# Two float32 blocks on one core: every second unit of weights is split by two loads instead of by DVE

## The chip, the cores and the metric

The kernel runs on one core of one Trainium2 chip. The metric is the device time of one execution in microseconds; the runs of a kernel are summed up by their median. One execution was recorded by the hardware profiler, and all rows below come from it.

## The reference

256 tokens of width 1024 go through two transformer-like blocks, all in float32:

```python
# first block
(q, kc, vc, ks, vs, kw, vw, nsa_g, rq, rk, rv, rg, gate_a, gate_b) = split(rmsnorm(x) @ w_in)
mix = sigmoid(gate_a) * (nsa_out @ w_proj_a) + sigmoid(gate_b) * (ret_out @ w_proj_b)
x = x + mix @ w_out
x = x + square(relu(rmsnorm(x) @ w_up)) @ w_down
x = rmsnorm(x)
# second block
h = x + hybrid_mixer(rmsnorm_2(x, ...), ...)          # SSD and gated linear attention
h = h + mem_cross_attention(rmsnorm_2(h, ...), rmsnorm_2(mem, ...), w_xq, w_xkv, w_xo)
h = h + swiglu(rmsnorm_2(h, ...), w_ffn_in, w_ffn_out)
return rmsnorm_2(h, norm_final)
```

Nearly all of the arithmetic is in the products with some 20 weight matrices, 163 MB in all, and every weight is used once for 256 tokens.

## The kernel before

TensorE multiplies operands of the type float32r, which has fewer bits than float32. So each float32 operand is split into two parts that are exact together: hi is the value rounded to float32r, lo is the value minus hi, rounded. A product of two operands takes three matrix products, hi x hi, hi x lo and lo x hi (the methods `tok_mm` and `feat_mm`, both through `mm`, line 104).

The weights come in 314 units of [128 partitions, 1024 columns], 512 KB (three of them smaller), which the host has laid out in `wbig` in the order of use. `load` (lines 87 to 97) fetches and splits one: SP's queue loads it into a buffer `raw` (line 93), ACT copies it to `wh` with rounding (line 94), and DVE subtracts `wh` from `raw` into `wl` (line 95). There are 4 buffers of `raw` and 8 each of `wh` and `wl`. So up to 8 units can be ready for TensorE and up to 4 more be on their way.

`gemm_tok` makes [128 tokens, 512 columns] from units of two blocks of 128 rows, once for each half of the tokens; `gemm_feat` makes [256 features, 256 tokens] from units of four blocks, and takes two units for 1024 rows, 48 matrix products. The `Down` class adds up the second matrix of an MLP, one unit for each 256 rows of it, 24 matrix products. The stages follow each other: the projections, the sparse attention (`nsa`) with other projections pumped in between, retention, the gated mix, the MLP of the first block (from 240 to 415 us), then the second block's projections, its two mixers, the cross attention, and its MLP to the end.

The activations are split in the same manner (`split`, line 111, ACT and then DVE). Before each of the large products stands a norm over the tokens: ACT squares and sums, DVE adds, GpSimd takes the power -1/2 (`rsqrt`, line 209), DVE scales, TensorE transposes, ACT and DVE split.

The order of the instructions on each engine is set when the program is built, by a scheduler with a model of the times; at run time each engine works off its own queue in order, and semaphores hold it where an operand isn't there yet. SP's queue holds nearly nothing but the 314 loads of weights. GpSimd's queue holds 27 loads (gains of the norms, the memory, decays, parameters), the powers of the norms, and some small operations. What `nc.gpsimd.dma_start` loads is moved by the same 16 DMA engines as SP's loads; GpSimd only issues it.

Of the kernel before, what the change touches and what calls it, by code (L numbers as in the profile page):

```python
# [19 lines left out]
P = 128  # L20
# [5 lines left out]
# columns of the packed constant array  # L26
C_ID, C_TRI, C_RST, C_INV, C_MC, C_AV, C_I94, C_BM, C_SEL, C_N = 0, 128, 256, 512, 584, 614, 616, 646, 654, 670
# packed parameters of the first block
A_PEK, A_PEV, A_CK2, A_CV2, A_N = 0, 16, 32, 288, 416
# packed parameters of the second block  # L30
B_CONV, B_BA, B_DTB, B_AL, B_D, B_A2, B_N = 0, 60, 64, 80, 96, 112, 624
# rows of gains
# [7 lines left out]
class Halves:  # L40
    """[128, 4 * n, 256 tokens], split in two exact parts, in tiles of four blocks each."""
# [8 lines left out]
class Builder:  # L50
# [35 lines left out]
    # ---- weights: loaded in units of up to half a megabyte, split into two parts that are exact together  # L86
    def load(self, w, c0, ncol, k, nk):
        nc = self.nc
        i = len(self.keys)
        self.keys.append((w, c0, ncol, k, nk))  # L90
        raw, wh, wl = self.T("raw", [P, UNIT]), self.T("wh", [P, UNIT], F32R), self.T("wl", [P, UNIT], F32R)
        m = nk * ncol
        nc.sync.dma_start(raw[:, :m], self.d["wbig"][i, :, :m])
        nc.scalar.copy(wh[:, :m], raw[:, :m])  # L94
        nc.vector.tensor_sub(wl[:, :m], raw[:, :m], wh[:, :m].bitcast(F32))  # L95
        cs = [slice(j * ncol, (j + 1) * ncol) for j in range(nk)]
        return [(wh[:, c], wl[:, c]) for c in cs]
# [23 lines left out]
    def gemm_tok(self, w, c0s, ncol, src, K=8, rest=None, mid=None, ahead=3, others=()):  # L121
        """[128 tokens, ncol] in one bank, for each group of columns and each half of the tokens; the first half of
        the tokens goes through all groups first, and rest makes the second half of src after that; mid takes the
        first half's results before the last group of the second."""
        us, n = [], UNIT // ncol
        for c0 in c0s:
            us.append([])
            for k in range(0, K, n):
                # all but the first weights are split after the first half of src
                with ExitStack() as order:  # L130
                    if rest and (c0 != c0s[0] or k >= ahead * n):
                        for x in self.first:
                            order.enter_context(self.tc.issue_after(x.ins))
                    us[-1] += self.load(w, c0, ncol, k, min(n, K - k))
                if c0 == c0s[0] and k // n in others:
                    others[k // n]()
# [10 lines left out]
    def s_tok(self, key, w, c0, ncol, src, done, K=8):  # L147
        """gemm_tok of one group of columns, in steps"""
# [17 lines left out]
    def s_feat(self, key, w, c0, src, done, K=8):  # L166
        """gemm_feat, in steps"""
# [18 lines left out]
    def gemm_feat(self, w, c0, src, K=8, tag="acc"):  # L186
        """[128 features, 2, 256 tokens]: two blocks of features in one bank."""
# [13 lines left out]
    def rstd(self, ssq, n, count, scale=1.0, eps=None):  # L201
        """1 / sqrt(scale * (ssq / count + eps))"""
# [9 lines left out]
    def norm_scale(self, src, junk):  # L212
        """1 / the root mean square of [128 tokens, 2 * 512]"""
# [7 lines left out]
    def norm_rows(self, src, g, out=None):  # L221
        """the norm of [128 tokens, 1024], in two tiles of 512 columns"""
# [8 lines left out]
    def norm_T(self, src, g, t, dst):  # L231
        """returns what is to be called for the transposes"""
# [7 lines left out]
    def norm_next(self, i, change):  # L240
        """the transposed norm of x as change leaves it, which calls its argument for each half of the tokens, and
        what is to be called for the second half of it"""
# [15 lines left out]
    def to_T(self, rows, t, dst, n=8, b0=0):  # L258
        """[128 tokens, n * 128] to the split [128, n, 128 tokens] at columns t."""
# [61 lines left out]
    def rope(self, out, x, t, nh, f0, nf, tmp):  # L321
        """out, x: [128 tokens, nh, 2, nf]; tmp [128, 2, nh, 2, nf]"""
# [15 lines left out]
    def compress(self, src, pe, w1, w2v, is_v):  # L338
        """src [128 = (token parity, dim), 2 groups, 256 tokens]"""
# [54 lines left out]
    def heads_T(self, kv, n, outs):  # L394
        """[128 tokens, n * 64]: each head, twice, transposed into the banks in outs"""
# [8 lines left out]
    def rope_T(self, acc):  # L404
        """rotary on four heads of 128, transposed: two tiles [128, 2 heads, 256 tokens]"""
# [21 lines left out]
    def silu2(self, acc, mul=None):  # L427
        """twice silu"""
# [24 lines left out]
    def nsa(self, hT, rest):  # L453
# [12 lines left out]
        # queries: two tiles of four heads; keys: [dim, branch, group, token]  # L466
# [12 lines left out]
        for t in range(2):  # L479
            ts = slice(t * P, (t + 1) * P)  # L480
            # keys and values of the compressed and the selected branch
# [13 lines left out]
            # queries  # L495
# [9 lines left out]
        for t in range(2):  # L505
            # window keys and values, gates
# [13 lines left out]
        # compressed attention  # L520
# [25 lines left out]
    def nsa_rest(self, kv_, gt, pcT, vbd):  # L546
        """selected and window attention, and the sum with the compressed one"""
# [140 lines left out]
    class Down:  # L688
        """x += u @ w: the blocks of u come one after the other, the last ones half of the tokens by half."""
# [15 lines left out]
        def rows(self, i, rows, scale):  # L705
            """four blocks, [128 tokens, 512] for each half of the tokens"""
# [11 lines left out]
        def feat(self, i, r, scale):  # L718
            """two blocks, [128 features, 2, 256 tokens]"""
# [4 lines left out]
        def go(self, n=1):  # L724
            """the products of the oldest blocks that wait"""
# [22 lines left out]
        def finish(self, then):  # L748
            """the rest, and then(t) for each half of the tokens"""
# [11 lines left out]
    def gated(self, gates, hT, aT, wa, Ka, bT, wb, Kb):  # L761
        """the split transpose of sigmoid(gate) * (a @ wa) + sigmoid(gate) * (b @ wb); the stream gives tanh(gate / 2)"""
# [22 lines left out]
    def residual(self, w, src, then):  # L785
        """x += src @ w, then(t) for each half of the tokens"""
# [8 lines left out]
    def dt_gate(self, hT, pb):  # L795
        """dt, its decays, and the transposed low-rank gate input."""
# [15 lines left out]
        # softplus: max(u, 0) + log1p(exp(-|u|)), log1p(e) = 2 atanh(e / (2 + e))  # L812
# [15 lines left out]
        # a = -exp(A_log) dt, its sums within each half, and their exponentials  # L828
# [21 lines left out]
        # the sums transposed, [head, token], in two parts that are exact together, one below the other  # L850
# [7 lines left out]
        # x, B and C come doubled  # L858
# [6 lines left out]
    def z_gate(self, hT, rest):  # L865
        """twice silu(z)"""
# [9 lines left out]
    def conv(self, pb, i, acc):  # L876
        """twice silu(conv(xBC)) for two blocks of features, [feature, 2, token]"""
# [42 lines left out]
    def ssd(self, hT, pb, dts, z, dec):  # L920
# [53 lines left out]
        def products(g, t, q):  # L974
# [18 lines left out]
            # the gate and the norm over the group  # L993
# [25 lines left out]
    def gla_decays(self, pb, a1T):  # L1019
        """exponentials of the sums of the log decays within chunks of 64 tokens, [dk, 2 heads, token], for each pair of  # L1020
        heads: for the queries, the keys, the keys towards the states, and each chunk's whole decay"""
# [11 lines left out]
        # one after the other, as they need another table  # L1033
# [18 lines left out]
    def gla(self, dec_):  # L1052
        """tiles of two chunks: the second chunk reads the first through their scores, and the second tile reads the
        first through one state"""
# [5 lines left out]
        for i in range(2):  # L1060
            v, r_ = self.need(f"v{i}"), self.need(f"r{i}")
            qt, kt, kh, dec = dec_[i]
            # scores, transposed: [key, head, query]
# [14 lines left out]
            # the state before the second tile, [dk, head, dv], and the queries that read it  # L1078
# [56 lines left out]
    def parts_of(self, src, scale=1.0, tags=("g2", "gd")):  # L1135
        """two tiles [128, 512] that make scale * src together"""
# [8 lines left out]
    def mm3(self, out, a, b, ca, cb, start, stop):  # L1145
        """out (+)= a[:, ca].T @ b[:, cb] of operands in two parts"""
# [110 lines left out]
def layout(inp):  # L1257
    """The inputs laid out for the loads; every value is copied as it is."""
# [91 lines left out]
```

## Time and profile before

| what | us |
|---|---|
| median of three runs (1007.6 to 1010.22) | 1008.44 |
| span of the profiled execution | 1007.4 |
| TensorE busy in it | 988.2 |
| DVE busy | 650.0 |
| ACT busy | 508.1 |
| GpSimd busy | 51.0 |

The profiled execution has no other time of its own than its span, from the first to the last instruction; it lies 1.0 us below the median of the runs. The granted clock of TensorE is at its full level from end to end (0.998 in the mean). 175.43 MB are moved by DMA, 174 GB/s in the mean, with the 16 DMA engines busy for about half of the time. Busy shares are read together with the list of waits: an engine that is busy for less than the span is late only where somebody waits for it.

### The profile page before, as it was taken

What the parts mean: (1) busy time and instruction counts of PE and PEld (TensorE: products, weight loads), DVE (VectorE), ACT (ScalarE), POOL (GpSimd) and SP (SyncE); (2) the same over time, 40 slices, a digit from 0 to 9 for tenths busy, and PEclk for the clock granted to TensorE, in tenths of its full rate; (3) what the DMA queues carried; (4) which work ended last, traced back from release to release, by engine and by line L of the source; (5) the groups of instructions that cost most, each with busy time, mean ns of one, the idle gap of its engine ahead of it and who ended that gap; (6) DMA issues with size and microseconds to landing.
All of it is one profiled execution on the core that took longest, in us unless ns stands there. A gap on an engine that the chain in (4) does not pass through costs nothing.

```text
span 1007.4 us, 16172 instructions
## 1 busy us (share of the span) xinstructions
PE 988.2 (98%) x6412; PEld 880.4 (87%) x6412; DVE 650.0 (65%) x959; ACT 508.1 (50%) x793; POOL 51.0 (5%) x77
## 2 busy tenths in 40 slices
PE   6999999999999999999999999999999999999997
PEld 5888998887888889789889899998998878999995
DVE  6897666666664555578778776576756466555543
ACT  5765445444554445465674555445545355444432
POOL 0000000000000000010000131200000000000000
PEclk9999999999999999999999999999999999999999
DMA  8758442333656575376445453753655156656531
GB/s 290 262 198 287 151 148 100 105 105 125 230 167 195 189 236 179 106 249 201 153 147 167 146 167 106 251 188 122 235 187 186 48 190 228 197 180 195 183 126 42
DMA packets 49547, 175.43 MB, mean 174 GB/s; under 512 B 5952, under 2 KB 6336, under 8 KB 49472
## 3 DMA queue, kind: packets, MB, share of 16 engines
q1 hardware_dynamic: 47088, 167.01, 50.5%
q0 software_dynamic: 2096, 6.87, 2.1%
q8 instruction: 50, 0.82, 0.3%
q10 hardware_dynamic: 288, 0.52, 0.1%
q14 instruction: 25, 0.20, 0.1%
HBM read 173.33 MB, written 1.05 MB: 173 GB/s over the span
## 4 chain that ended last, share of the span: by engine, by line
PE 96%; DMA 2%; ACT 1%; issue 1%; DVE 0%; SPq 0%; POOLq 0%; POOL 0%; ACTq 0%
PE acc L104 68%; PE sm L104 23%; PE sm L108 3%; PE po L104 2%; DMA raw<-in_wbig_dram 2%; ACT wh L94 1%; ACT hh L111 0%; DVE wl L95 0%; SPq L198 0%; SPq L276 0%; DVE k L1251 0%; ACT g L269 0%; POOLq L1344 0%; POOL sc L209 0%; SPq L280 0%
## 5 line engine op out<-in xcount | busy, mean ns | idle before, releaser
L95 DVE TENSOR_TENSOR wl<-raw,wh 128x1024 fp32r<-128x1024 f32 (+1 forms) x314 | 381.7, 1227 | 222.6 <-ACT wh L94 221.8
L94 ACT CAST wh<-raw 128x1024 fp32r<-128x1024 f32 (+1 forms) x314 | 325.6, 1048 | 304.3 <-PE acc L104 141.9
L104 PE MATMUL acc<-hh,wh 128*128 128x256 f32 x736 | 207.6, 283 | 0.4 <-ACT hh L111 0.4
L104 PE MATMUL acc<-hl,wh 128*128 128x256 f32 x736 | 207.8, 283 | 0.0
L104 PE MATMUL acc<-hh,wl 128*128 128x256 f32 x736 | 207.4, 282 | 0.0
L104 PE MATMUL acc<-wh,hh 128*128 128x512 f32 (+1 forms) x400 | 156.7, 397 | 1.9 <-ACT hh L111 1.9
L104 PE MATMUL acc<-wl,hh 128*128 128x512 f32 (+1 forms) x400 | 157.3, 395 | 0.0
L104 PE MATMUL acc<-wh,hl 128*128 128x512 f32 (+1 forms) x400 | 155.9, 397 | 0.0
L104 PEld LDWEIGHTS acc<-hh,wh 128*128 128x128 f32 x736 | 138.0, 188 | 1.7 <-ACT hh L111 0.5
L104 PEld LDWEIGHTS acc<-hl,wh 128*128 128x128 f32 x736 | 138.3, 188 | 0.9 <-issue 0.7
L104 PEld LDWEIGHTS acc<-hh,wl 128*128 128x128 f32 x736 | 138.1, 188 | 0.4 <-issue 0.3
L104 PE MATMUL sm<-hh,wl 128*128 128x256 f32 x488 | 136.4, 280 | 0.0
L104 PE MATMUL sm<-hl,wh 128*128 128x256 f32 x488 | 136.4, 279 | 0.0
L104 PE MATMUL sm<-hh,wh 128*128 128x256 f32 x488 | 136.2, 279 | 0.0
L104 PEld LDWEIGHTS acc<-wh,hh 128*128 128x128 f32 x400 | 75.8, 190 | 19.5 <-ACT hh L111 3.2
L104 PEld LDWEIGHTS sm<-hl,wh 128*128 128x128 f32 x488 | 91.6, 188 | 0.8
L104 PEld LDWEIGHTS sm<-hh,wh 128*128 128x128 f32 x488 | 91.5, 187 | 0.9
L104 PEld LDWEIGHTS acc<-wh,hl 128*128 128x128 f32 x400 | 75.7, 189 | 18.2 <-DVE hl L111 1.2
L104 PEld LDWEIGHTS sm<-hh,wl 128*128 128x128 f32 x488 | 91.5, 187 | 0.0
L104 PEld LDWEIGHTS acc<-wl,hh 128*128 128x128 f32 x400 | 75.7, 189 | 16.6 <-DVE wl L95 0.5
L104 PE MATMUL acc<-wh,gd 128*128 128x512 f32 x216 | 85.3, 396 | 1.6 <-ACT gd L699 1.2
L104 PE MATMUL acc<-wl,gd 128*128 128x512 f32 x216 | 84.8, 393 | 0.0
(272 smaller groups left out, 1058.0 us busy)
## 6 DMA issues: line engine op xcount, KB each, us to landing
raw<-in_wbig_dram SPq DMA_DIRECT2D x311, 512.0 KB, 4.0
k<-in_gains_dram POOLq DMA_DIRECT2D x18, 256.0 KB, 4.3
k<-in_mem_dram POOLq DMA_DIRECT2D x4, 256.0 KB, 6.4
raw<-in_wbig_dram SPq DMA_DIRECT2D x2, 420.0 KB, 3.8
k<-in_decay_dram POOLq DMA_DIRECT2D x4, 192.0 KB, 4.9
xr<-in_x_dram SPq DMA_DIRECT2D x2, 256.0 KB, 2.7
k<-in_gains_dram SPq DMA_DIRECT2D x2, 256.0 KB, 5.2
xr<-in_x_dram SPq DMA_DIRECT2D x1, 512.0 KB, 7.6
```

The costliest lines, as they stand in the source:

```text
L94: nc.scalar.copy(wh[:, :m], raw[:, :m])
L95: nc.vector.tensor_sub(wl[:, :m], raw[:, :m], wh[:, :m].bitcast(F32))
L104: self.nc.tensor.matmul(out, lhsT, rhs, start=start, stop=stop)
L108: self.nc.tensor.transpose(out, src, self.ident[:n, :n])
```

## The change

For the odd units from number 17 on, 149 of the 314, there is no `raw` buffer and nothing on SP's queue or on DVE. GpSimd's queue loads the unit straight into `wh`, a float32r tile, so that the load rounds. ACT then writes `wl` = -`wh`. After that GpSimd's queue loads the same unit from HBM a second time, with an addition: `wl` = `wl` + unit. The even units and the first 16 are fetched and split as before, and the matrix products are the same. (The comments and docstrings were also taken out of the file, and lines after `load` stand 8 lower.)

```diff
-        raw, wh, wl = self.T("raw", [P, UNIT]), self.T("wh", [P, UNIT], F32R), self.T("wl", [P, UNIT], F32R)
         m = nk * ncol
-        nc.sync.dma_start(raw[:, :m], self.d["wbig"][i, :, :m])
-        nc.scalar.copy(wh[:, :m], raw[:, :m])
-        nc.vector.tensor_sub(wl[:, :m], raw[:, :m], wh[:, :m].bitcast(F32))
+        src = self.d["wbig"][i, :, :m]
+        if i % 2 and i >= 16:
+
+            wh, wl = self.T("wh", [P, UNIT], F32R), self.T("wl", [P, UNIT], F32R)
+            nc.gpsimd.dma_start(wh[:, :m], src)
+            nc.scalar.activation(wl[:, :m], wh[:, :m].bitcast(F32), AF.Copy, scale=-1.0)
+            nc.gpsimd.dma_start(wl[:, :m], src, accum_op=OP.add)
+        else:
+            raw, wh, wl = self.T("raw", [P, UNIT]), self.T("wh", [P, UNIT], F32R), self.T("wl", [P, UNIT], F32R)
+            nc.sync.dma_start(raw[:, :m], src)
+            nc.scalar.copy(wh[:, :m], raw[:, :m])
+            nc.vector.tensor_sub(wl[:, :m], raw[:, :m], wh[:, :m].bitcast(F32))
```

The scheduler places the new instructions. On GpSimd before, from the loads of the gains for the norm ahead of the first MLP to the loads for the norms behind it (L198 loads gains, L209 is the power of a norm):

```order
L198 DMA k_532_2428<-in_gains_dram 128x512
L198 DMA k_533_2429<-in_gains_dram 128x512
L209 TENSOR_TENSOR sc_2569<-sc_2567,mhalf_74 128x1
L209 TENSOR_TENSOR sc_2620<-sc_2618,mhalf_74 128x1
L198 DMA k_832_4118<-in_gains_dram 128x512
L198 DMA k_833_4119<-in_gains_dram 128x512
```

On GpSimd now, at the two powers of that norm (L96 is the rounding load, L98 the accumulating load of the unit whose `wh` has the number one lower, L217 the power):

```order
L96 DMA wh_2599<-in_wbig_dram 128x1024
L98 DMA wl_2600<-in_wbig_dram 128x1024
L96 DMA wh_2610<-in_wbig_dram 128x1024
L217 TENSOR_TENSOR sc_2544<-sc_2542,mhalf_74 128x1
L98 DMA wl_2611<-in_wbig_dram 128x1024
L96 DMA wh_2621<-in_wbig_dram 128x1024
L96 DMA wh_2632<-in_wbig_dram 128x1024
L217 TENSOR_TENSOR sc_2595<-sc_2593,mhalf_74 128x1
L98 DMA wl_2622<-in_wbig_dram 128x1024
L98 DMA wl_2633<-in_wbig_dram 128x1024
```

Where GpSimd had the two powers alone, loads now stand before and between them, and the first accumulating load stands right behind the rounding load of its own unit. In the dense part of the same MLP, where GpSimd's queue was empty, it now holds:

```order
L96 DMA wh_3355<-in_wbig_dram 128x1024
L96 DMA wh_3397<-in_wbig_dram 128x1024
L98 DMA wl_3356<-in_wbig_dram 128x1024
L98 DMA wl_3398<-in_wbig_dram 128x1024
L96 DMA wh_3457<-in_wbig_dram 128x1024
L96 DMA wh_3499<-in_wbig_dram 128x1024
L98 DMA wl_3458<-in_wbig_dram 128x1024
L98 DMA wl_3500<-in_wbig_dram 128x1024
```

There two rounding loads stand side by side ahead of their two accumulating loads. ACT's queue in the same part (L94 and L102 round a unit of the old kind, L97 makes -`wh`, L676 and L684 are the relu of a group, L111 and L119 the rounding of its square), before:

```order
L94 CAST wh_3298<-raw_3297 128x1024
L94 CAST wh_3335<-raw_3334 128x1024
L94 CAST wh_3341<-raw_3340 128x1024
L94 CAST wh_3396<-raw_3395 128x1024
L94 CAST wh_3402<-raw_3401 128x1024
L676 ACTIVATE k_701_3327<-sm_3206 128x512
L111 CAST gd_3330<-k_701_3327 128x512
```

and now:

```order
L97 ACTIVATE wl_3254<-wh_3253 128x1024
L102 CAST wh_3301<-raw_3300 128x1024
L97 ACTIVATE wl_3296<-wh_3295 128x1024
L102 CAST wh_3361<-raw_3360 128x1024
L684 ACTIVATE k_662_3288<-sm_3169 128x512
L119 CAST gd_3291<-k_662_3288 128x512
L97 ACTIVATE wl_3356<-wh_3355 128x1024
```

Every second rounding copy has become a multiplication that waits for a load of GpSimd's queue.

## Rows read from the trace of the kernel before

**Rows 1.** The page, part 1: busy us (share of the span) and instructions by engine.

```profile
PE 988.2 (98%) x6412; PEld 880.4 (87%) x6412; DVE 650.0 (65%) x959; ACT 508.1 (50%) x793; POOL 51.0 (5%) x77
```

**Rows 2.** Waits of TensorE, longest first: us in total, times, longest us.

```profile
PE sm L108 <- DMA cst<-in_cst_dram: 7.9, 1, 7.9
PE acc L104 <- ACT hh L111: 2.2, 6, 0.8
```

**Rows 3.** Busy us by stretch: length, engines (instructions), clock, DMA share, GB/s.

```profile
core 0: us, PE busy (x) PEld busy (x) DVE busy (x) ACT busy (x) POOL busy (x), PEclk, DMA share, GB/s
0.00:50.00 50.00, 41.31 (x196) 34.23 (x197) 37.63 (x85) 34.41 (x57) 1.31 (x6) 1.00 0.81 276
50.00:100.00 50.00, 50.00 (x270) 42.41 (x269) 40.01 (x73) 31.60 (x56) 2.34 (x4) 1.00 0.72 242
...
250.00:300.00 50.00, 49.59 (x293) 43.45 (x293) 29.86 (x35) 26.56 (x36) 0.00 (x0) 1.00 0.61 204
300.00:400.00 100.00, 100.00 (x644) 90.49 (x643) 54.17 (x53) 46.02 (x53) 2.19 (x4) 1.00 0.63 204
400.00:450.00 50.00, 49.41 (x229) 39.88 (x228) 33.74 (x41) 26.33 (x42) 4.24 (x6) 1.00 0.51 164
450.00:500.00 50.00, 50.00 (x358) 45.39 (x357) 40.97 (x82) 29.99 (x48) 2.07 (x2) 1.00 0.60 188
...
600.00:650.00 50.00, 50.00 (x425) 48.45 (x424) 31.01 (x49) 25.48 (x40) 9.08 (x16) 1.00 0.55 184
...
700.00:750.00 50.00, 50.00 (x405) 48.89 (x405) 33.87 (x37) 26.12 (x34) 0.55 (x1) 1.00 0.67 220
...
800.00:850.00 50.00, 48.54 (x247) 40.39 (x246) 34.58 (x42) 27.33 (x37) 1.11 (x2) 1.00 0.56 189
850.00:950.00 100.00, 100.00 (x716) 93.84 (x716) 52.72 (x54) 42.86 (x47) 0.00 (x0) 1.00 0.60 190
950.00:1007.00 57.00, 50.16 (x333) 45.56 (x331) 24.89 (x31) 18.76 (x27) 1.10 (x2) 0.96 0.28 93
```

**Rows 4.** The page, part 5: group | busy us, mean ns | idle before.

```profile
L95 DVE TENSOR_TENSOR wl<-raw,wh 128x1024 fp32r<-128x1024 f32 (+1 forms) x314 | 381.7, 1227 | 222.6 <-ACT wh L94 221.8
L94 ACT CAST wh<-raw 128x1024 fp32r<-128x1024 f32 (+1 forms) x314 | 325.6, 1048 | 304.3 <-PE acc L104 141.9
```

**Rows 5.** The chain that ended last, 320 to 360 us: start us, us.

```profile
344.40 5.66 PE sm L104 x48
350.05 5.56 PE acc L104 x24
```

**Rows 6.** Groups by shape, two of ACT of 128x512.

```profile
L111 ACT CAST hh<-sm 128x512 fp32r<-128x512 f32 x38 | 21.4, 586 | 27.8 <-PE sm L108 23.3 <-PE sm L104 4.3
L269 ACT ACTIVATE g<-acc 128x512 f32<-128x512 f32 x26 | 15.4, 594 | 8.4 <-PE acc L104 5.7 <-PE sm L104 1.7 <-DVE k L1112 0.9
```

**Rows 7.** Line 198 on GpSimd: duration of the issue, ns min/median/max, first and last start.

```profile
L198 POOL DMA_DIRECT2D k<-in_gains_dram x18: 536/537/609, 186.7 to 770.4; - x18
```

**Rows 8.** The page, part 3: DMA queue, packets, MB, share of 16 engines.

```profile
q1 hardware_dynamic: 47088, 167.01, 50.5%
q0 software_dynamic: 2096, 6.87, 2.1%
```

**Rows 9.** Busy us by stretch, the first 18 us alone.

```profile
0.00:18.00 18.00, 9.31 (x30) 6.99 (x31) 9.26 (x16) 9.91 (x18) 1.31 (x6) 1.00 0.88 309
```

**Rows 10.** The page, part 6: DMA issues, KB each, median us to landing.

```profile
raw<-in_wbig_dram SPq DMA_DIRECT2D x311, 512.0 KB, 4.0
k<-in_gains_dram POOLq DMA_DIRECT2D x18, 256.0 KB, 4.3
k<-in_mem_dram POOLq DMA_DIRECT2D x4, 256.0 KB, 6.4
```

**Rows 11.** Waits of all engines: GpSimd's longest.

```profile
POOL sc L209 <- DVE sc L218: 426.1, 16, 178.4
```

## The prediction

> **What bounds the kernel now.** I read the share of busy time first, then what TensorE waited for, then the table by stretch, then the chain of work in one dense stretch, then the DMA queues and issues. TensorE is busy for 98% of the span; DVE, which the change relieves, for 65% and ACT for 50% [rows 1]. The list of waits gives TensorE one long wait, 7.9 us for the first constants at the start, and then 2.2 us in six pieces [rows 2]. By stretch it is short of work only at the two ends: 8.7 us are missing in the first 50 us and 6.8 us in the last 57 us [rows 3]. What is left over is 1007.4 - 988.2 - 8.7 - 6.8 = 3.7 us. The reader is to see in this that there is next to nothing to win: what DVE and ACT do for the weights is already hidden behind TensorE. DVE idles 221.8 us before its weight subtractions, waiting for ACT, and nobody is late for it [rows 4].
>
> In the MLP of the first block the chain is TensorE alone: 48 matrix products in 5.66 us, 24 in 5.56 us [rows 5]. 48 products are one group of features, that is two units of weights. So where the weights come densely, TensorE eats two units in 5.65 us, and from now on one of the two is of the new kind.
>
> **What the change takes away.** 149 units (every odd one from 17 to 313) lose a subtraction on DVE, 1227 ns each [rows 4]: 183 us of DVE time. None of it is on the chain, so it is worth nothing in itself. SP loses 149 loads. ACT keeps its time: the rounding copy of 1048 ns [rows 4] becomes a multiplication by -1 of the same size, and in this trace a plain activation of 128x512 takes 594 ns where a rounding copy of that size takes 586 [rows 6]. I take the two as equal, 0 us.
>
> **What it adds.** Two loads on GpSimd's queue in place of one on SP's: 298 issues there, where the kernel before has 27. Issuing one takes GpSimd 537 ns (a 256 KB load) [rows 7]; 298 x 0.54 = 161 us on an engine that is busy for 51 us. That lies beside everything else, except for the order, below. What counts is the DMA engines. 167.01 MB of hardware-queue traffic took 50.5% of the 16 engines' span, 3.05 us per MB; 6.87 MB on GpSimd's queue took 2.1%, 3.08 us per MB [rows 8]. So a plain load of 512 KB costs 1.6 us of all 16 engines on either queue, and I charge the rounding load the same. The accumulating load appears nowhere in this trace. It must fetch the source, fetch its destination and write the sum. Its lower bound is one load (1.6 us, the second fetch free). Two loads (3.2 us) is what it takes if the second fetch costs what the first does together with its write. Three is the upper bound, each of the three passes as long as a whole load. Below nothing no end can lie, since the bytes are moved a second time. I take two, because the fetch of the destination is real work on the same engines and the row nearest to it is that of a plain load.
>
> The Trainium skill ("Collectives: The Full Stack", section "The bandwidth ceiling: the fold count and why AG ≠ RS ≠ AR") says that an adding DMA is slower for its two source reads, not for the addition, and gives a ratio of 1.93. No row here shows it; by that figure the sum by shares below would be 106 us where mine is 118.
>
> Per stretch the share of the DMA engines now becomes: half the units as before, half with one rounding load and one accumulating load. With an accumulate of two loads that is (0.5 + 0.5 x 3) = 2.0 times the share; with one load 1.5 times; with three 2.5 times. Where the product is over 1, the stretch must grow by the excess, because eight buffers of each part are only some 8 x 2.83 = 23 us of lead. By the nine stretches whose share is over one half [rows 3], the factor 2.0 gives 22 (50 to 100 us) + 11 (250 to 300) + 26 (300 to 400) + 1 (400 to 450) + 10 (450 to 500) + 5 (600 to 650) + 17 (700 to 750) + 6 (800 to 850) + 20 (850 to 950) = 118 us. A share may overstate what is needed, since packets that wait for each other last longer: in the first 18 us the engines move 309 GB/s at a share of 0.88 [rows 9], 351 GB/s if full. Doubling the GB/s of the same nine stretches and dividing by 351 gives 19 + 8 + 16 + 0 + 4 + 2 + 13 + 4 + 8 = 74 us. I take the middle of 74 and 118, 96 us. Bounds: the factor 1.5 gives 4 us (only 50 to 100 us, 1.08, is over), the factor 2.5 gives 286 us from the same nine stretches.
>
> **The order on GpSimd.** Its queue is worked off in order, and an accumulating load waits for ACT's multiplication, which waits for the rounding load to land. In the dense stretch of the MLP two loads and two accumulates alternate, so one landing covers two units. But 36 of the 149 accumulates stand right behind their own load (as in the second piece of the order shown above). There GpSimd stands still from the issue to ACT's end, and the next rounding load is queued behind it. Such a pair lasts two issues, a landing and one ACT step: 1.07 + 4.3 + 1.05 = 6.4 us with the landing of a 256 KB gain, 8.5 us with the 6.4 us of those that were issued in a row [rows 10], against TensorE's 5.65. That is 0.8 to 2.9 us each, 27 to 103 us in all if no lead absorbs it. Where the DMA engines are short anyway it is the same wait and isn't added; where they are not, TensorE's lead of several units absorbs single pairs. In the forecast it counts 0; it is the price of a rival. ACT waits in order too: its multiplication stands ahead of the relu of the next group, so a late rounding load delays ACT's other work. GpSimd's small powers for the norms (26 of them, 0.6 us) now stand between loads; before, GpSimd idles 426.1 us ahead of 16 of them [rows 11], so they started at once. Of a norm TensorE waits for the result.
>
> **The sum.** The profiled execution's span is 1007.4 us, the median of the runs 1008.4, 1.0 above. 1008.4 + 96 (DMA engines) + 0 (DVE, ACT, SP) = 1104, rounded 1105 us.
>
> **Rivals.** *One load's price, and GpSimd's order binds.* If the accumulate costs one load, the engines give 4 us, and the 36 pairs that stand alone give 27 or more: 1008.4 + 4 + 27 = about 1040, from 1016 to 1080. For it: the two queues cost the same per MB. Against it: the destination must be fetched. *Three passes.* 1008.4 + 286 = 1294; then the DMA engines, not TensorE, bound nearly every stretch with weights. For it: no row bounds the accumulate better. *All hidden.* One load's price and all pairs absorbed: 1009 to 1016. *Faster.* DVE has 183 us less in its queue, so what waits for DVE in the norms and the attention comes earlier, and TensorE closes its gaps between the stages. The price is the 3.7 us left over above: 1004.7. It decides only if the accumulate costs less than about one load and no norm on GpSimd is late; the gaps that are seen wait for ACT at least as much as for DVE [rows 2]. That the change doesn't do what it says (DVE's 149 subtractions still there) is excluded by the order, which has 150 DVE rows fewer.
>
> **How the numbers follow.** A measurement of this kernel can tell about 0.3%, 3 us, from no change. Two loads' price, 1080 to 1180 us: 0.42. One load's price with GpSimd's order binding, 1016 to 1080: 0.20. Three passes or near, 1180 to 1320: 0.20, and 0.03 beyond. All hidden, 1009 to 1016: 0.09, of which two thirds end within 0.3%. Faster: 0.06. The first three hold 0.82, so the range goes from 1016 to 1300. Faster by over 0.3%: 0.06; within: 0.06; slower: 0.88.
>
> **What would show it.** Right, if in the changed profile the DMA share stands at 0.9 or more through 300 to 400 us and the last MLP, GpSimd's queue takes some 20% or more of the engines per 78 MB of rounding loads and about twice that for as much of accumulates, TensorE's busy share falls below 92%, and TensorE's waits name the second part or its DMA. The order on GpSimd is the cause instead if the DMA share stays under 0.85 while TensorE waits, and GpSimd's own list of waits is led by ACT's multiplication. Wrong from the start, if TensorE still shows no wait in those stretches: then the accumulate costs less than a load, and the time is 1004 to 1016.

## The result and the profile after

| | before | changed |
|---|---|---|
| median us (three runs) | 1008.44 | 1186.95 (1183.33 to 1189.16) |
| ratio, 95% interval | 1 | 1.176 (1.1737 to 1.1784) |
| span of the profiled execution | 1007.4 | 1181.6 |
| TensorE's mean granted clock | 0.998 | 0.951 |

The change costs 178.5 us; the forecast was 97. Part 1 of the page, part 3, one group of part 5 and two rows of part 6, for the changed kernel, answer to [rows 1, 8, 4, 10]; L96 is the rounding load, L97 ACT's multiplication, L98 the accumulating load:

```profile
PE 1046.7 (89%) x6412; PEld 915.3 (77%) x6412; DVE 486.5 (41%) x810; ACT 498.3 (42%) x793; POOL 263.2 (22%) x375
...
q0 software_dynamic: 45008, 163.13, 58.5%
q1 hardware_dynamic: 25632, 88.88, 21.3%
...
L97 ACT ACTIVATE wl<-wh 128x1024 fp32r<-128x1024 f32 x149 | 157.7, 1059 | 450.8 <-DMA wh<-in_wbig_dram 424.0
...
wh<-in_wbig_dram POOLq DMA_DIRECT2D x149, 512.0 KB, 7.1
wl<-in_wbig_dram POOLq DMA_DIRECT2D x149, 512.0 KB, 6.0
```

DVE has lost 163.5 us of work and the kernel gained nothing by it. The same 6412 matrix products keep TensorE busy for 1046.7 us, 58.5 more than before, and it stands idle for 1181.6 - 1046.7 = 134.9 us where it was 19.2. Together 58.5 + 115.7 = 174.2 us, the whole growth of the span. So there are two things to explain: the idle time, and why the same products became longer.

The waits of all engines (us in total, times, longest us), which answer to [rows 2, 11]:

```profile
POOL wl L98 <- ACT wl L97: 547.4, 122, 12.8
ACT wl L97 <- DMA wh<-in_wbig_dram: 424.0, 107, 15.8
...
POOL wh L96 <- PE acc L112: 194.7, 49, 28.7
...
PEld acc L112 <- DMA wl<-in_wbig_dram: 51.4, 21, 6.0
...
PE acc L112 <- DMA wl<-in_wbig_dram: 44.5, 20, 5.8
```

Read from below: TensorE and its weight loads wait for second parts to land, the accumulating loads wait 547 us for ACT, and ACT waits 424 us for rounding loads. That is a chain. It is not all that TensorE waits for: of the 124 us in its list of waits 62.0 are for second parts, 5.8 for first parts and 8.2 for the first constants; the other 48 are for activations that ACT or DVE had not ready (4 us in the kernel before). That the DMA engines are not simply full is a first reading of the table by stretch of the first MLP (columns as in [rows 3]):

```profile
300.00:350.00 50.00, 45.82 (x273) 40.21 (x272) 15.11 (x21) 19.30 (x27) 9.89 (x14) 0.97 0.87 235
350.00:400.00 50.00, 41.65 (x240) 35.66 (x239) 13.42 (x14) 16.63 (x20) 10.63 (x16) 0.97 0.83 213
400.00:450.00 50.00, 42.36 (x235) 36.65 (x234) 10.88 (x12) 16.29 (x20) 8.55 (x12) 0.90 0.83 229
```

From 300 to 400 us 273 + 240 = 513 products are done where there were 644 [rows 3], while the DMA engines stand at 0.87 and 0.83. The loop that sets the pace in the second half is seen on GpSimd (start us, us, what, and in brackets how long the engine stood before it and for whom):

```profile
349.19 0.88 POOL L98 DMA_DIRECT2D wl<-in_wbig_dram  x1 [7.45 <-ACT wl L97]
351.09 0.88 POOL L98 DMA_DIRECT2D wl<-in_wbig_dram  x1 [1.02 <-ACT wl L97]
351.64 1.45 POOL L96 DMA_DIRECT2D wh<-in_wbig_dram  x2
363.39 0.88 POOL L98 DMA_DIRECT2D wl<-in_wbig_dram  x1 [10.31 <-ACT wl L97]
365.28 0.87 POOL L98 DMA_DIRECT2D wl<-in_wbig_dram  x1 [1.01 <-ACT wl L97]
365.83 1.44 POOL L96 DMA_DIRECT2D wh<-in_wbig_dram  x2
```

and on ACT in between:

```profile
362.03 1.06 ACT L97 ACTIVATE wl<-wh 128x1024 fp32r<-128x1024 f32 x1 [8.44 <-DMA wh<-in_wbig_dram]
363.00 1.03 ACT L102 CAST wh<-raw 128x1024 fp32r<-128x1024 f32 x1
363.93 1.05 ACT L97 ACTIVATE wl<-wh 128x1024 fp32r<-128x1024 f32 x1
```

Two rounding loads are issued at 351.64. ACT can start on the first only at 362.03: beside the two accumulates issued just ahead of it, it takes over 10 us to land. (Over the whole kernel the median is 7.1 us; with plain loads in place of the accumulates, in the first experiment below, it is 5.1.) ACT takes 1.06, and at 363.39 GpSimd, which stood for 10.31 us, issues the accumulate, after ACT's second multiplication the other one, and only then, at 365.83, the next two rounding loads. One turn is 365.83 - 351.64 = 14.2 us and brings four units (the two even ones come beside it by SP); the next three, to 380.64, 395.14 and 409.91, are 14.8, 14.5 and 14.8. TensorE eats four units in 5.66 + 5.56 = 11.2 us [rows 5]. 11.2 over the mean turn of 14.6 is 0.77; from 350 to 400 us 240 products are done where half of the 644 were done before, 0.75. The next rounding loads don't wait for a buffer here; they wait for their turn in the queue. That is so from 351 us on: from 300 to 350 us rounding loads still wait for TensorE to free a buffer, and 0.85 of the products are done. A turn that is longer than TensorE's uses up the lead of eight buffers and doesn't win it back.

**The longer products.** Around two such waits in the same MLP, by short stretches (columns as in [rows 3]), and four of the products of 128x512 there:

```profile
398.00:402.00 4.00, 4.00 (x18) 3.23 (x18) 0.00 (x0) 0.00 (x0) 0.00 (x0) 1.00 1.03 278
...
408.00:412.40 4.40, 1.23 (x10) 0.91 (x8) 3.62 (x4) 2.52 (x4) 1.98 (x3) 1.00 0.95 144
412.40:415.90 3.50, 3.44 (x10) 2.71 (x11) 0.00 (x0) 0.00 (x0) 0.00 (x0) 0.63 0.99 250
415.90:419.00 3.10, 3.10 (x13) 2.47 (x12) 0.00 (x0) 0.00 (x0) 0.00 (x0) 0.87 1.06 394
419.00:424.00 5.00, 5.00 (x42) 4.89 (x41) 1.95 (x3) 4.47 (x6) 1.60 (x3) 1.00 0.55 126
```

```profile
397.74 0.50 PE L112 MATMUL acc<-wl,gd 128*128 128x512 f32 x1 [2.96 <-DMA wl<-in_wbig_dram]
...
412.46 0.51 PE L112 MATMUL acc<-wl,gd 128*128 128x512 f32 x1 [3.23 <-DMA wl<-in_wbig_dram]
412.81 0.40 PE L112 MATMUL acc<-wh,k 128*128 128x512 f32 x1
...
414.08 0.63 PE L112 MATMUL acc<-wh,gd 128*128 128x512 f32 x1
```

At the second wait TensorE stood for 3.23 us, then ran three products at the full 2.4 GHz, and then the granted clock fell, 0.63 and 0.87 in the mean of two stretches, 1.2 GHz for part of each; a product shows 0.63 us where it shows 0.40. After some 3 us it was back. So a stall can be paid a second time, but not every one is: the first wait, of 2.96 us, is followed by no fall (1.00 from 398 to 402 us). Over the span the mean clock gives (0.998 - 0.951) x 1181.6 = 56 us for it, near the 58.5 us by which TensorE's busy time grew.

### The profile page after: what moved, and what is told of

It is laid out like the page before. It is cut to its first block, busy times and chain, and to the rows that moved or that the text cites. A ratio compares the mean times of both kernels' runs of the same rounds, so it can differ in the third digit from the quotient of the medians.

```text
span 1181.6 us, 16130 instructions
## 1 busy us (share of the span) xinstructions
PE 1046.7 (89%) x6412; PEld 915.3 (77%) x6412; DVE 486.5 (41%) x810; ACT 498.3 (42%) x793; POOL 263.2 (22%) x375
## 3 DMA queue, kind: packets, MB, share of 16 engines
q0 software_dynamic: 45008, 163.13, 58.5%
HBM read 251.45 MB, written 1.05 MB: 214 GB/s over the span
## 4 chain that ended last, share of the span: by engine, by line
issue 34%; PE 26%; DMA 24%; POOL 10%; ACT 3%; DVE 2%; POOLq 0%; SPq 0%; ACTq 0%; DVEq 0%
PE acc L112 19%; DMA wh<-in_wbig_dram 15%; DMA wl<-in_wbig_dram 8%; PE sm L112 5%; POOL wl L98 4%; POOL wh L96 4%; ACT wl L97 2%; POOL sc L217 1%; DMA raw<-in_wbig_dram 1%; DVE wl L103 1%; PE sm L116 1%; DMA k<-in_gains_dram 0%; POOL k L973 0%; POOL g L443 0%; ACT wh L102 0%
## 5 line engine op out<-in xcount | busy, mean ns | idle before, releaser
L97 ACT ACTIVATE wl<-wh 128x1024 fp32r<-128x1024 f32 x149 | 157.7, 1059 | 450.8 <-DMA wh<-in_wbig_dram 424.0
L103 DVE TENSOR_TENSOR wl<-raw,wh 128x1024 fp32r<-128x1024 f32 (+1 forms) x165 | 212.0, 1291 | 223.3 <-ACT wh L102 223.0
L98 POOL DMA_DIRECT2D wl<-in_wbig_dram x149 | 130.4, 877 | 620.1 <-ACT wl L97 547.4
L112 PE MATMUL acc<-hh,wh 128*128 128x256 f32 x736 | 212.6, 290 | 3.9 <-ACT g L431 3.5
L102 ACT CAST wh<-raw 128x1024 fp32r<-128x1024 f32 (+1 forms) x165 | 170.1, 1039 | 89.9 <-PE acc L112 52.0
L112 PE MATMUL acc<-wl,hh 128*128 128x512 f32 (+1 forms) x400 | 162.1, 407 | 18.4 <-DMA wl<-in_wbig_dram 18.4
L96 POOL DMA_DIRECT2D wh<-in_wbig_dram x149 | 102.7, 722 | 226.9 <-PE acc L112 194.7
L112 PEld LDWEIGHTS acc<-hh,wl 128*128 128x128 f32 x736 | 142.6, 194 | 6.9 <-DMA wl<-in_wbig_dram 6.4
L112 PEld LDWEIGHTS acc<-hh,wh 128*128 128x128 f32 x736 | 142.5, 194 | 5.9 <-ACT g L431 3.7
L112 PE MATMUL acc<-wl,gd 128*128 128x512 f32 x216 | 90.5, 421 | 20.6 <-DMA wl<-in_wbig_dram 20.6
```

The lines of the kernel that those rows point to most:

```text
L96: nc.gpsimd.dma_start(wh[:, :m], src)
L97: nc.scalar.activation(wl[:, :m], wh[:, :m].bitcast(F32), AF.Copy, scale=-1.0)
L98: nc.gpsimd.dma_start(wl[:, :m], src, accum_op=OP.add)
L112: self.nc.tensor.matmul(out, lhsT, rhs, start=start, stop=stop)
```

## The experiments

Two theories stood against each other. **Price:** the second pass over the weights, and the accumulate above all, fills the DMA engines (the forecast). **Loop:** GpSimd's queue, in which an accumulate stands still until its own load has landed, with the next loads behind it. (The expectations also call them volume and order.) Times are medians; the kernel before gave 1008.7 to 1009.6 beside them.

**Accumulate replaced by a plain load, order on every engine unchanged.**

```diff
-            nc.gpsimd.dma_start(wl[:, :m], src, accum_op=OP.add)
+            nc.gpsimd.dma_start(wl[:, :m], src)
```

> The second load of an odd unit is a plain one, which overwrites the negative; so its second part is the whole weight, and the output is another. The order on every engine is that of the changed kernel, so only the accumulate's price is taken away. If the accumulate occupies the DMA engines twice as long as a load (packets of 318 ns against 159 ns), the rounding load queued behind two of them lands some 2.5 to 3 us earlier, GpSimd's loop of 14.4 us for four units falls to 11 to 12 us against TensorE's 11.3, and the time is 1030 to 1080 us. If the price of the accumulate does not matter and only the chain load, ACT, load does, the time stays over 1150. If volume alone matters (three loads for two units), 1009 to 1020.

Measured: 1046.96 us, ratio 1.039 (1.034 to 1.045). 140 us go with the accumulate alone, though every engine's order is the same. GpSimd in the same stretch:

```profile
350.13 0.53 POOL L96 DMA_DIRECT2D wh<-in_wbig_dram  x1 [4.23 <-PE sm L112]
352.86 0.53 POOL L98 DMA_DIRECT2D wl<-in_wbig_dram  x1 [2.20 <-ACT wl L97]
355.39 0.53 POOL L98 DMA_DIRECT2D wl<-in_wbig_dram  x1 [1.99 <-ACT wl L97]
...
361.37 0.53 POOL L96 DMA_DIRECT2D wh<-in_wbig_dram  x1 [4.30 <-PE sm L112]
```

Now the rounding loads wait for TensorE to free a buffer, and a turn is 361.37 - 350.13 = 11.2 us, TensorE's own pace. So the order alone does not cost it; the accumulate is needed too.

**Chain cut, accumulate kept.** ACT writes zeros that depend on no load.

```diff
-            nc.scalar.activation(wl[:, :m], wh[:, :m].bitcast(F32), AF.Copy, scale=-1.0)
+            nc.scalar.activation(wl[:, :m], self.ones[:, 0:1].broadcast_to((P, m)), AF.Copy, scale=0.0)
```

> ACT writes zeros into the second part from a constant, so neither ACT nor the accumulating load waits for the rounding load; the accumulating load and all bytes stay, and the second part is the whole weight. Order theory (GpSimd stands still for a landing of 7 to 10 us and an ACT step, and the next rounding load is queued behind): the wait is gone, 1010 to 1060 us. Volume theory (the DMA engines are simply too slow for accumulates of twice a load): still 1105 to 1190 us, DMA share 0.9 or more in the dense stretches.

Measured: 1047.51 us, ratio 1.037 (1.035 to 1.040). 139 us go, with every accumulate there. Not the wait alone is gone, however: the scheduler made the order anew. In GpSimd's queue, which had two accumulates and then two rounding loads in the dense part, the two kinds now alternate (in the first MLP L96 at 356.29, L98 at 357.15, L96 at 361.12, L98 at 362.33). The first MLP:

```profile
300.00:350.00 50.00, 50.00 (x318) 45.02 (x317) 16.20 (x17) 23.15 (x27) 12.88 (x19) 1.00 0.99 266
350.00:400.00 50.00, 50.00 (x316) 44.97 (x315) 17.24 (x19) 23.94 (x28) 12.65 (x18) 1.00 1.05 280
```

TensorE never stops, with all accumulates there and the DMA engines at 0.99 and 1.05. They are full, but what they have to move in this MLP is not more than they can. This speaks against the price theory, which had put 26 us on these 100.

**Both.**

```diff
-            nc.scalar.activation(wl[:, :m], wh[:, :m].bitcast(F32), AF.Copy, scale=-1.0)
-            nc.gpsimd.dma_start(wl[:, :m], src, accum_op=OP.add)
+            nc.scalar.activation(wl[:, :m], self.ones[:, 0:1].broadcast_to((P, m)), AF.Copy, scale=0.0)
+            nc.gpsimd.dma_start(wl[:, :m], src)
```

> Both at once: zeros from ACT and a plain second load, order as in e2; the second part is the whole weight. Both theories: 1005 to 1020 us. What is left over 1008 here is neither the chain nor the accumulate's price but the moved order on the other engines.

Measured: 1021.07 us, ratio 1.012 (1.010 to 1.013). The four corners:

| us | no chain | chain |
|---|---|---|
| plain second load | 1021.1 | 1047.0 |
| accumulate | 1047.5 | 1187.0 |

The two cells of each column have the same order on every engine; the columns differ in the wait and in the order that the scheduler made for it. Moving the bytes a second time costs 12, whatever the new order on the other engines costs included; the chain with its order by itself costs 26, the accumulate by itself 26, and the two together 113.6 more than the sum (1187.0 - 1047.0 - 1047.5 + 1021.1).

**The same work in another order.** The strongest test keeps the multiplication with its wait, the accumulate and the result, and asks for a rounding load earlier, by one odd unit (end i + 3) or by two (end i + 5). The scheduler places the rest anew here too.

```diff
-            wh, wl = self.T("wh", [P, UNIT], F32R), self.T("wl", [P, UNIT], F32R)
-            nc.gpsimd.dma_start(wh[:, :m], src)
+            for j in range(i, min(i + 5, NUNITS), 2):
+                if j not in self.early:
+                    self.early[j] = self.T("wh", [P, UNIT], F32R)
+                    nc.gpsimd.dma_start(self.early[j], self.d["wbig"][j])
+            wh, wl = self.early.pop(i), self.T("wl", [P, UNIT], F32R)
```

> The same bytes, the same multiplication on ACT and the same accumulate as in the changed kernel, and the full result. Only the rounding load of an odd unit is now asked for one odd unit earlier, so that GpSimd's queue reads load n+2, accumulate n, load n+4, accumulate n+2, where two loads stood ahead of two accumulates. Loop theory (what costs 140 us is that GpSimd stands at an accumulate whose own load has only just been issued, with the next loads behind it): the wait of the accumulates for ACT falls from 547 us to under 350 and the time to 1050 to 1120. Rival, the moved bytes alone, in whatever order: 1175 to 1200. Rival, the wh buffers are held for one odd unit longer, so the lead shrinks: over 1190.

> As the run before, with the rounding load asked for two odd units earlier. Loop theory: the wait of the accumulates for ACT falls further, 1040 to 1090; not below the 1047 of the run that kept the accumulates and had no chain, but for some us. Moved bytes alone: 1175 to 1200. Buffers held longer: slower than the run with one odd unit of lead.

Measured: one ahead 1144.91 us, ratio 1.134 (1.129 to 1.140), outside all three brackets, and the accumulates still wait 474.3 us for ACT where under 350 was expected; two ahead 1047.96, ratio 1.039 (1.0375 to 1.041), the time of the kernel without a chain. With two ahead, the waits and the first MLP:

```profile
POOL wh L99 <- PE acc L116: 309.2, 88, 27.8
POOL wl L102 <- ACT wl L101: 253.4, 80, 11.0
...
ACT wl L101 <- DMA wh<-in_wbig_dram: 34.9, 20, 6.4
```

```profile
300.00:350.00 50.00, 50.00 (x306) 44.56 (x306) 16.62 (x18) 23.24 (x28) 12.71 (x18) 1.00 1.03 279
350.00:400.00 50.00, 50.00 (x317) 44.99 (x316) 16.92 (x20) 23.13 (x28) 12.65 (x18) 1.00 1.03 281
```

ACT's wait for rounding loads falls from 424.0 to 34.9 us, and GpSimd now waits longest for TensorE, which frees the buffers. 139 of the 178.5 us are the order, with the same bytes, accumulates and arithmetic; 51.0 of them are TensorE's products, which are shorter again (1046.7 to 995.7 us). The changed kernel's order on the other engines doesn't explain it by itself: the first experiment has that order on every engine and took 1047.0 us. With one ahead the first MLP is at full speed as well, but the last, from 910 us on, is not (the table, and GpSimd there):

```profile
350.00:400.00 50.00, 50.00 (x318) 45.02 (x317) 16.57 (x17) 21.50 (x25) 11.81 (x17) 1.00 1.03 277
...
1000.00:1050.00 50.00, 37.70 (x240) 33.62 (x240) 10.95 (x12) 14.52 (x17) 8.56 (x12) 0.87 0.80 218
```

```profile
997.36 1.41 POOL L99 DMA_DIRECT2D wh<-in_wbig_dram  x2
...
1019.63 0.86 POOL L102 DMA_DIRECT2D wl<-in_wbig_dram  x1 [10.36 <-ACT wl L101]
1020.18 1.43 POOL L99 DMA_DIRECT2D wh<-in_wbig_dram  x2
```

So one odd unit of lead is a pace near TensorE's own, kept in one place and lost in another. Where it is lost the loop is back: GpSimd stands 10.36 us at an accumulate, with two rounding loads behind it. What brings it back in the last MLP was not tried.

**More buffers in place of another order.**

```diff
-    raw=4, wh=8, wl=8, hh=5, hl=5, xr=2, g2=9, k2=14, gd=9, sc=32,
+    raw=2, wh=9, wl=9, hh=5, hl=5, xr=2, g2=9, k2=14, gd=9, sc=32,
```

> Nine buffers of each part in place of eight, two raw buffers in place of four; every load as in the changed kernel. Loop theory: in the dense stretches GpSimd's period of 14.4 us for four units does not depend on how many buffers there are, since the rounding loads there wait for no buffer but for their place behind the accumulates: 1150 to 1190 us. Lead theory (TensorE waits because a unit is asked for too late): each unit of lead more is worth 2.83 us per wait, and the time falls below 1130.

Measured: 1156.35 us, ratio 1.146 (1.142 to 1.151). That is inside the bracket of the loop theory, and GpSimd still waits 561.8 us for ACT ahead of its accumulates. But it is 31 us better, with a buffer more for each part (paid with two of `raw`), which the loop theory didn't foresee. The scheduler made the order anew here as well, so the 31 us can't be put to the buffers alone.

**Each load by itself.** Accumulate alone (the odd units' rounded part as before, from `raw`), and rounding load alone (the second part as before, from `raw`):

```diff
-            nc.gpsimd.dma_start(wh[:, :m], src)
+            nc.sync.dma_start(raw[:, :m], src)
+            nc.scalar.copy(wh[:, :m], raw[:, :m])
```

> Odd units are loaded by SP's queue into a raw buffer and rounded by ACT, ACT negates, and GpSimd's queue holds the accumulating loads alone; the bytes and the accumulates stay, ACT gets 149 steps of 1.06 us more. Order theory: no load stands behind a waiting accumulate any more, so 1010 to 1060 us. Volume theory: the engines move as much as in the changed kernel, 1105 to 1190 us.

```diff
-            nc.scalar.activation(wl[:, :m], wh[:, :m].bitcast(F32), AF.Copy, scale=-1.0)
-            nc.gpsimd.dma_start(wl[:, :m], src, accum_op=OP.add)
+            nc.sync.dma_start(raw[:, :m], src)
+            nc.vector.tensor_sub(wl[:, :m], raw[:, :m], wh[:, :m].bitcast(F32))
```

> Odd units get their first part from the rounding load on GpSimd's queue, a raw copy from SP's queue, and their second part from DVE's subtraction as before: three plain loads for two units, no accumulate, no ACT step for odd units, and nothing on GpSimd waits for a load. Order theory: the rounding load is harmless by itself, 1008 to 1025 us, near the 1021 of the kernel with neither chain nor accumulate. If rounding in the load has a price of its own (its landing in the changed kernel was 7.1 us against 4.0 of a plain load before), over 1030.

Measured: accumulate alone 1054.28 us, ratio 1.046 (1.043 to 1.049); rounding load alone 1040.88, ratio 1.0325 (1.028 to 1.037), more than expected and in the bracket of a price for rounding. GpSimd's queue in the one (span 1049.0 us),

```profile
q0 software_dynamic: 23552, 85.00, 41.5%
```

and its queue and ACT's longest wait in the other (span 1034.7 us):

```profile
q0 software_dynamic: 23552, 85.00, 25.6%
```

```profile
ACT wh L102 <- DMA raw<-in_wbig_dram: 193.8, 62, 8.2
```

Of the 85.00 MB, 6.87 are the loads of before, at 3.08 us per MB 21 us [rows 8]. The 149 accumulates then take 0.415 x 1049.0 - 21 = 414 us of all 16 engines, 2.78 us each; the 149 rounding loads 0.256 x 1034.7 - 21 = 244 us, 1.64 each. So rounding costs the DMA engines nothing, 1.64 us against the 1.6 of a plain load, and an accumulate costs 1.7 loads, where the forecast had two. The Trainium skill ("Collectives: The Full Stack", "The bandwidth ceiling: the fold count and why AG ≠ RS ≠ AR") gives a ratio of 1.93 for an add in a collective, which it puts down to two source reads; measured here, for loads into SBUF, is 1.7. The rounding load alone costs 32 us, more than the 12 of as many bytes in the kernel with neither chain nor accumulate; ACT stands in order there for `raw` that SP fetches, and whether that is the cause was not tested.

**Fewer new units.**

```diff
-        if i % 2 and i >= 16:
+        if i % 4 == 1 and i >= 16:
```

> The change for every fourth unit only, 75 units in place of 149. If each unit costs the same (178 us over 149 units, 1.2 us each): 1098 us. Loop theory: a chain load, ACT, accumulate of 9 to 10 us then stands against TensorE's 11.3 us for four units and hides: 1010 to 1035 us, that is, far less than half of the loss.

```diff
-        if i % 2 and i >= 16:
+        if i % 32 == 17:
```

> The change for one unit in 32, 10 units, so that each accumulating load stands nearly alone. Time 1006 to 1011 us by the loop theory, 1020 if each unit cost 1.2 us. What it is for: the landing of an undisturbed rounding load and of an undisturbed accumulating load of 512 KB, and of its packets. If the accumulate reads its destination on the same engines, packets of 318 ns against 159 ns here too, and a landing 1.3 to 1.8 us above the rounding load's.

Measured: 75 new units 1059.46 us, ratio 1.052 (1.048 to 1.055); ten 1024.05, ratio 1.0155 (1.014 to 1.017). Both are misses: ten units cannot form a loop nor fill the DMA engines, and cost 15 us, 1.5 each. So a third cause was there. (The ten accumulates take a median of 5.3 us to land, 1.0 more than the ten rounding loads, where 1.3 to 1.8 was expected. Most of their packets of 4096 bytes take 328 ns in the trace, with ten new units as with 149, and most of the rounding loads' 174.) ACT in the kernel with ten, at the start of the MLP:

```profile
265.15 1.04 ACT L102 CAST wh<-raw 128x1024 fp32r<-128x1024 f32 x1
271.00 1.06 ACT L97 ACTIVATE wl<-wh 128x1024 fp32r<-128x1024 f32 x1 [4.80 <-DMA wh<-in_wbig_dram]
271.96 1.97 ACT L102 CAST wh<-raw 128x1024 fp32r<-128x1024 f32 x2
273.84 0.64 ACT L119 CAST gd<-sm 128x256 fp32r<-128x256 f32 x2
```

ACT stands for 4.80 us at a multiplication whose load is still on its way, and the rounding of the activations (`gd`, L119) stands behind it; TensorE waits 3.1 us for that `gd`. Two runs tell this from its rivals: ten plain loads moved to GpSimd with the rest of the kernel before as it is, and the ten new units with their rounding load asked for four units earlier.

```diff
-        nc.sync.dma_start(raw[:, :m], self.d["wbig"][i, :, :m])
+        (nc.gpsimd if i % 32 == 17 else nc.sync).dma_start(raw[:, :m], self.d["wbig"][i, :, :m])
```

> The kernel before, with ten of its 314 plain loads (every 32nd unit, the ten that the run with one unit in 32 treated anew) issued by GpSimd in place of SP; ACT's, DVE's and TensorE's orders are word for word those of before, and the result is full. If the 15 us of the run with ten new units come from what stands on GpSimd's queue, 1015 to 1025. If they come from ACT's wait for a second load, the accumulate, or from the order that the scheduler made anew on ACT and TensorE: 1007 to 1012.

```diff
+        if i % 32 == 13 and i + 4 < NUNITS:
+            self.early[i + 4] = self.T("wh", [P, UNIT], F32R)
+            nc.gpsimd.dma_start(self.early[i + 4], self.d["wbig"][i + 4])
         if i % 32 == 17:
-            wh, wl = self.T("wh", [P, UNIT], F32R), self.T("wl", [P, UNIT], F32R)
-            nc.gpsimd.dma_start(wh[:, :m], src)
+            wh, wl = self.early.pop(i), self.T("wl", [P, UNIT], F32R)
```

> The kernel with ten new units (every 32nd), whose rounding load is asked for four units earlier; full result. There ACT waited for the ten loads, 22.4 us, with other work of ACT queued behind each wait, and the kernel was 15 us over the one before; merely moving ten plain loads to GpSimd cost 0.8 us. If the 15 us are ACT's waits for loads that were asked for too late, the waits go to under 5 us and the time to 1009 to 1015. If they come from the ten accumulates themselves, or from the order that the scheduler made anew for ACT and TensorE, it stays at 1019 to 1027.

Measured: moved loads 1009.92 us, ratio 1.0008 (0.9999 to 1.0018); load ahead 1009.18, ratio 1.000 (0.999 to 1.001). The same multiplication with its load ahead:

```profile
263.54 1.06 ACT L100 ACTIVATE wl<-wh 128x1024 fp32r<-128x1024 f32 x1 [0.23 <-DMA wh<-in_wbig_dram]
...
269.98 0.64 ACT L122 CAST gd<-sm 128x256 fp32r<-128x256 f32 x2
```

It waits 0.23 us in place of 4.80, and the activations' rounding starts at 269.98 in place of 273.84. Over the kernel ACT's waits for the ten loads fall from 22.4 us to 0.2, and the 15 us are gone: they came from loads that were asked for too late. Ten accumulates with their loads in time cost nothing that can be measured. The scheduler's order differs between these two kernels in other places too, so its share is not told apart by itself. Why 75 new units cost 51 us was not followed up; the same two waits lead there, 404.0 us of accumulates for ACT and 191.3 us of ACT for rounding loads. No version beat the kernel before: with its load in time the new unit is free at best, since DVE, which it relieves, is nobody's bound.

## Why the prediction was right or wrong

- **Nothing to win** (DVE's 183 us worthless, ACT equal): right. DVE is busy for 486.5 us in place of 650.0, with 149 instructions fewer (the prediction's 150 is one too many), and nobody gained; the multiplication takes 1059 ns against the copy's 1048 [rows 4].
- **Issues on GpSimd, 298 x 0.54 us, beside other work**: too low. The 298 issues take 130.4 + 102.7 = 233 us and not 161, since issuing an accumulate takes GpSimd a median of 875 ns where a plain second load takes 530, and the rounding loads 765 where they take 537 beside plain second loads. GpSimd is busy for 263.2 us, 22% of the span, so this alone is no bound.
- **The accumulate as two loads, 3.2 us**: somewhat high; 2.78, 1.7 loads.
- **The DMA engines, 96 us**: mis-sized. The second pass and the accumulates cost 12 + 26 = 38 us where the order doesn't interfere. The step that failed is the multiplication of shares. It gave 0.63 x 2.0 = 1.26 and 26 us for 300 to 400 us; measured, with every accumulate there and TensorE at full speed, is 1.03. Two of its factors were too high. With an accumulate of 1.7 loads the factor is 1.87. And only the weights are multiplied: the 36 units fetched in these 100 us are 18.9 of the 20.4 MB that were moved, so 0.63 counts too much. 0.63 x 18.9 / 20.4 x 1.87 is 1.09; the last 0.06 stay open. And at 1.03 TensorE lost nothing, so a share a little over 1 need not lengthen a stretch. The prediction's doubt, that waiting packets swell the share, does not explain it: in these 100 us plain and rounding loads take 3.1 us of all engines per MB before, and 3.1 in the kernel with neither chain nor accumulate. The prediction took the middle of two readings, both of them too high.
- **GpSimd's order counts 0**: the step that failed most. It is 139 of the 178.5 us. The text had the parts (an accumulate waits for ACT, ACT for the landing, the next load stands behind), but priced only the 36 accumulates that stand right behind their own load, and took "one landing covers two units" as the end of it in the dense stretch. It put a landing of at most 6.4 us into the turn. There a turn is 14.2 to 14.8 us for four units, because a landing beside two accumulates takes some 10; summed up as a period it would have been 3.0 to 3.6 us over TensorE's 11.2. (The 36 is right, by the trace; the accumulates whose own load is the last one issued ahead of them are 80.)
- **"Where the DMA engines are short anyway it is the same wait and isn't added"**: the reverse. The slow accumulates lengthen the landing that the order then waits for, so each makes the other dearer: 26 and 26 by themselves, 113.6 more together.
- **ACT waits in order too**: named without a price. It is 1.5 us for each of ten single units, 15 in all; in the changed kernel TensorE's waits for activations grow from 4 to 48 us, and how much of that is ACT's order is not shown.
- **TensorE's clock** does not stand in the sum. 58.5 us of the growth is TensorE's own products, which take longer; the mean clock gives 56 of it to the lower level after its waits.
- **What would show it:** TensorE below 92% (89) and its waits name the second part: as said. The DMA share was to be 0.9 or more for the forecast, under 0.85 with ACT's multiplication leading GpSimd's waits for the rival. It is 0.87 and 0.83 from 300 to 400 us and 0.87 and 0.88 in the last MLP (1000 to 1100 us), mostly between the two marks, so the share alone decides little; the list of waits, led by ACT's multiplication with 547.4 us, pointed to the rival, rightly. The rounding loads were to take some 20% of the engines and the accumulates twice that: measured alone 244 us and 414 us, 24% and 39% of their spans.

So the direction, the place and the waits were right, and the split was not: 96 + 0 + 0 was forecast, and it is 38 for the engines and 139 for the order, part of it as lost clock. That the range holds the measured time is luck in good part. 1187 us lies above the 1080 to 1180 of the mechanism that was forecast, in the bracket of three passes, and three passes are excluded, since an accumulate takes 1.7 loads. The rival whose mechanism came nearest, GpSimd's order, had 1016 to 1080 us and was tied to an accumulate of one load. Open is what exactly the 39 us of the version with two units of lead are: its profile, which is 36.5 us longer, shows 18.2 us of TensorE's waits for second parts, 8.4 for DVE ahead of a transpose (line 240) and 7.5 us of longer products (995.7 against 988.2); the rest is in small pieces.

## What to carry to other kernels

Where a queue that is worked off in order issues a step that needs an earlier step's landing, write down the period of that queue: issues, landing under load, the engine between, and hold it against the period of the consumer. If it is longer, one more buffer helped little here (31 of 178.5 us) and asking for the first load two steps earlier helped most (139). An engine's queue with one such wait and other work behind it is read in the same way. Two costs that meet in one chain (a slower transfer, a queue that waits for it) don't cover each other; here they cost more together than their sum.

## What the runs showed of the hardware

An accumulating load of 512 KB takes 2.78 us of all 16 DMA engines where a rounding or a plain one takes 1.6, and it also takes GpSimd longer to issue. The second load in the changed kernel, and in the one where it is plain (duration of the issue, ns min/median/max, first and last start):

```profile
L98 POOL DMA_DIRECT2D wl<-in_wbig_dram x149: 846/875/1192, 52.2 to 1161.6; - x149
```

```profile
L98 POOL DMA_DIRECT2D wl<-in_wbig_dram x149: 527/530/617, 51.7 to 1021.9; - x149
```

A rounding load costs the engines what a plain one costs (1.64 and 1.6 us). The granted clock fell to its lower level shortly after a wait of only 3.2 us, when the products were running again, and came back some 3 us later; after a wait of 2.96 us it did not fall. The busy share of the DMA engines, as the profile gives it, can stand a little over 1: 1.03 and 1.05 over 50 us, with TensorE busy all the time.
